# Rooms for every block of x, key and query weights on ScalarE's queue, chunks that end where blocks end

## The chip, the core and the metric

One core of a Trainium2 chip runs the kernel. The metric is device time of one execution in microseconds (us). The kernel before took 1500.04 us, the median of three runs (1497.89 to 1501.41).

TensorE (PE) does matmuls, VectorE (DVE) and GpSimd (POOL) elementwise work, ScalarE (ACT) copies, casts and activations; SyncE (SP) issues loads and stores, which 16 DMA engines carry out. Each engine works through its own list of instructions in order.

## The reference

Two layers over 1040 tokens (16 learned meta tokens, then 1024 of x) of width 1024; everything is float32.

```python
def hybrid_layer(h, ...):
    u = rms_norm(h, norm_g)
    proj = jnp.einsum('bld,dp->blp', u, w_in)          # 1024 x 4104
    dq, dk, dv, dz, fq, fk, fv, fz, f_logit = jnp.split(proj, split_points, axis=-1)
    # 4 differential heads: rope(q1), rope(q2), rope(k1), rope(k2), d = 64, v 128 wide
    #   p = softmax(q1 k1) - lam * softmax(q2 k2); o_a = rms_norm(p @ v_a) * (1 - lambda_init)
    # 8 forgetting heads, d = 64: softmax(q k / 8 + c_q - c_k) @ v, c = cumsum(log_sigmoid(f_logit + b))
    mixed = jnp.concatenate([o_a * jax.nn.silu(dz), o_b * jax.nn.silu(fz)], axis=-1)
    return h + jnp.einsum('bld,dm->blm', mixed, w_out)

out = rms_norm(h, final_g)[:, 16:]
```

## The kernel before, in words

**Precision.** A float32 product is made of three fast ones: each operand is split into a high part (a cast to fp32r) and the low rest. So a projection of one column block of 128 takes 24 matmuls per chunk of tokens: for each of the 8 slices of the width `XTh*whi`, `XTh*wlo` and `XTl*whi`. POOL splits weights (L314 high, L317 low, for quarters of 256 rows); ACT and DVE split x.

**The head of layer 0.** x is loaded in 8 blocks of 128 tokens (`hb`), block 0 being the 16 meta tokens. They are normed in three groups (`GRPS`: blocks 0 to 2, 3 to 5, 6 to 8): ACT squares each with a running sum (L256), DVE makes the factors of a group in a chain of small steps (L257, L231 to L244) and norms each block with the gain `gb` into `u` (L267). PE transposes `u` in halves (L282), ACT casts each half into `XTh` (L292), DVE subtracts the rest into `XTl` (L293).

**Unit 0.** Eight units (four differential heads, four pairs of forgetting heads) follow each other; unit 0's key, query and value projections (L341, L406) stand before its attention, and the next unit's projections are woven between its attention's steps by the scheduler. A projected key or query takes rope: ACT casts the chunk into `raw` (L491), SP copies its halves crosswise into `sw` (four copies, once for the first two chunks and once for the third), DVE multiplies by the cosine (L500), POOL `sw` by the sine (L501), DVE adds (L502), ACT and DVE split (L515, L508), and for the query SP copies the high part to the other half of the partitions (`qa`). The first matmul of an attention is L799 (meta tokens).

**Order and rooms.** Nobody writes the order: the framework's scheduler runs the program in a model of time and lists each engine's instructions by it. A tile names a tag with a number of rooms; where the rooms lie, and which earlier tile's place a new one takes, is decided in the same run, and the instruction that fills a tile then waits for the last readers of what lay there. `e` has 4 rooms and five blocks of x ask for one, so block 5 takes the room of block 1. Every load signals one of eight semaphores (DMAHW0 to 7), given in turn in that order, and waits until the load that had it before has landed.

SP's list begins with seven blocks of x, meta and gb, then `wf` (weights of the forget gates, 32 bytes a row), `gsc` (a small table), the key weights of unit 0 (L302, four quarters), its query weights (four), the rope tables, and block 5.

Of the kernel before, what the change touches and what calls it, by code (L numbers as in the profile page):

```python
# [12 lines left out]
F32 = mybir.dt.float32  # L13
# [6 lines left out]
P = 128  # L20
NM = 16
SEQ = 1024
L = NM + SEQ
D = 1024
KT = D // P
# [7 lines left out]
ST = 3  # L33
NE = 4
# [1 line left out]
MW = 584  # L36
AHEAD = 3
XORD = (1, 0, 2, 3, 4, 5, 6, 7, 8)
W0 = 8
ON_POOL = ()  # L40
SPL_POOL = ()
GRPS = ((0, 1, 2), (3, 4, 5), (6, 7, 8))
# [7 lines left out]
WLB = 6  # L50
VPB = 0
STB = 3
NQZ = 3
PMB = 4
OTB = 2
# [15 lines left out]
SH = 0  # L71
PP = ()
WARM = 20
CKB = False
KR = True
PG = ()
AQ = True
AV = True
WQ0 = False
WQ1 = False  # L80
CORD = (1, 0, 2, 3)
PSB = (0, 0, 0, 0)
Z_AT = {0: [0], 1: [1], 2: [2], 4: [3], 7: [4, 5, 6, 7]}
# [30 lines left out]
def hybrid_kernel(ctx: ExitStack, tc: tile.TileContext, x, meta, norm_g, w_in, b_forget,  # L114
                  lam_q1, lam_k1, lam_q2, lam_k2, subln_g, w_out, final_g, cos_t, sin_t, out):
    nc = tc.nc
# [5 lines left out]
    wp = Sized(ctx.enter_context(tc.tile_pool(name="wp", bufs=3)))  # L122
# [48 lines left out]
    def slot(nm):  # L171
        r = rings[nm]
        c = r[0] + r[3] % r[1] * r[2]
        r[3] += 1
        return cst[:, c:c + r[2]]
# [117 lines left out]
                nc.vector.tensor_tensor(out=lv, in0=psv, in1=hv.bitcast(F32), op=ALU.subtract)  # L293


    def load_w(l, col, q=None, room=None, rawroom=None):

        his, los = [], []
        raws = []
        for qt in range(4 if rawroom else 0):  # L300
            raws.append(rawroom(qt))
            (q or nc.sync).dma_start(out=raws[-1], in_=w_in[l, 256 * qt:256 * qt + 256, col:col + P].rearrange("(k p) c -> p k c", p=P))  # L302
        for qt in range(4):
          if rawroom:
            raw = raws[qt]
          else:
            raw = wp.tile([P, 2, P], F32, name="wraw", tag="wlo", bufs=WLB or None)
            (q or nc.sync).dma_start(out=raw, in_=w_in[l, 256 * qt:256 * qt + 256, col:col + P].rearrange("(k p) c -> p k c", p=P))
          if room is not None:
            hi, lo = room[:, qt], room[:, 4 + qt]  # L310
          else:
            hi = wp.tile([P, 2, P], F32R, name="whi", tag="whi", bufs=WHB or None)
            lo = None
          nc.gpsimd.tensor_scalar(out=hi, in0=raw, scalar1=1.0, scalar2=1.0, op0=ALU.mult, op1=ALU.mult)  # L314
          if lo is None:
            lo = wp.tile([P, 2, P], F32R, name="wlo", tag="wlo", bufs=WLB or None)
          nc.gpsimd.tensor_tensor(out=lo, in0=raw, in1=hi.bitcast(F32), op=ALU.subtract)  # L317
          his.append(hi)
          los.append(lo)
        return his, los  # L320
# [6 lines left out]
    ahead = {}  # L327
# [3 lines left out]
            late.pop(0)()  # L331

    def proj(l, col, chunks, evac):
        his, los = ahead.pop((l, col), None) or load_w(l, col, nc.scalar if (WQ1 and l == 0 and col % 512 == 0 and col < 2048) else None)
        for t0, n in chunks:
            ps = pj(f"pj_{l}_{col}")
            cnt = 0
            for k in range(KT):
                hi, lo = his[k // 2][:, k % 2, :], los[k // 2][:, k % 2, :]
                for w, xx in ((hi, XTh), (lo, XTh), (hi, XTl)):  # L340
                    nc.tensor.matmul(ps[:, :n], lhsT=w, rhs=xx[:, k, t0:t0 + n],  # L341
                                     start=(cnt == 0), stop=(cnt == 23))
                    cnt += 1
            run_late()
            evac(ps, t0, n)
            yield 24 * n / 2370.0
# [124 lines left out]
    def unit_proj(l, j, U, tabs):  # L471
        diff = j < 4
        cq, ck, cv, _ = unit_cols(j)
        tq = 0 if l == 0 else NM
        ch_q = CH_ALL if l == 0 else CH_REAL
        U.diff, U.j, U.l, U.tq = diff, j, l, tq
        lowhalf, tophalf = slice(0, 64), slice(64, 128)
        halves = (lowhalf, tophalf)
# [43 lines left out]
        def split_k(src, c0, scale, t0, n):  # L522
            for m in range(2):
# [1 line left out]
                hi = U.K1[m][halves[m], t0:t0 + n]  # L525
                hi_part(hi, x, scale)
                sub(U.K1[m][halves[1 - m], t0:t0 + n], x, scale, hi, f'k{m}')
        yield from project(ck, CH_BLK if CKB and l == 0 and j == 0 else CH_ALL, 0, 1.0, split_k)
        if not diff and KE:
            U.Kb = []  # L530
            for m in range(2):
# [409 lines left out]
    dma(bfb, bcast_rows(b_forget, P))  # L941
    hbs = {}
    gb = None
    htags = [("st", ST)] + [("e", NE)] * 5 + [("st", ST)] * 2 + [("ot", OTB)]
    for i, b in enumerate(XORD):
        t0, n = blk(b)
        tg, nb = htags[b]
        hb = big.tile([P, L], F32, name="hb", tag=tg, bufs=nb or None)[:, :D]
        dma(hb[:n], meta if b == 0 else x2[P * (b - 1):P * b])
        hbs[b] = (hb, n)  # L950
        if i == 0:
            gb = big.tile([P, L], F32, name="gb", tag="ot", bufs=OTB or None)[:, :D]
            dma(gb, bcast_rows(norm_g[0], P))
        if i == W0:
            ck0 = unit_cols(0)[1]
            ahead[0, ck0] = load_w(0, ck0, nc.scalar if WQ0 else None, None, (lambda qt: wp.tile([P, 2, P], F32, name="wraw", tag="wlo", bufs=WLB or None)) if KR else None)
    utags = ("k0", "k1", "qa0", "qa1") * 2 + ("ql",)
    for grp in GRPS:
        us = [stk.tile([P, L], F32, name="u", tag=utags[b])[:, :D] for b in grp]
# [9 lines left out]
    def prefetch(l, todo):  # L969

        for w in todo:
            col = unit_cols(0)["qkv".index(w)]
            if w == "k":
                ahead[l, col] = load_w(l, col)
            if w == "q":
                room = vp.tile([P, NB, 2, P], F32R, name="wroom", tag="V")
                ahead[l, col] = load_w(l, col, None, room,
                                       lambda qt: slot("es")[:, :256].rearrange("p (k c) -> p k c", k=2))
            if w == "v":
                ahead[l, "v"] = load_v01(l)  # L980

# [190 lines left out]
```

## Time and profile before

| | |
|---|---|
| median of three runs | 1500.04 us |
| the profiled execution | 1498.74 us |
| its span | 1497.1 us |
| PE busy | 1419.0 us, 95% |
| DVE, ACT, POOL busy | 955.3, 699.9, 627.8 us |
| L341 matmuls (projections) | 3 x 1392, about 452 us each third |
| chain that ended last | PE 75%, DVE 8%, DMA 5%, SP's queue 4% |

The span is cut into 40 slices of 37 us; the page's row of PE reads 28899..., so only the first slice shows PE mostly idle. A busy share over all 1497 us says nothing about that slice; it is read from its own rows below.

### The profile page before, as it was taken

How to read it: one execution, taken by the hardware profiler on the slowest of the kernel's cores; microseconds unless marked ns; L12 is line 12 of the kernel's file. 1: busy time of each engine (PE TensorE's matmuls, PEld its weight loads, DVE VectorE, ACT ScalarE, POOL GpSimd, SP SyncE). 2: the span in 40 equal slices, each digit the busy share in tenths (PEclk: the TensorE clock that was granted, in tenths of full speed). 3: DMA queues.
4: the chain of work that ended last, by engine and by line, in shares of the span. 5: the costliest groups of instructions: out<-in, count | busy, mean ns of one | idle time of the engine just before them, and what ended most of it. 6: DMA issues, size and time to landing. Idle time of an engine off the chain costs nothing.

```text
span 1497.1 us, 26781 instructions
## 1 busy us (share of the span) xinstructions
PE 1419.0 (95%) x9262; PEld 1348.8 (90%) x9262; DVE 955.3 (64%) x2721; ACT 699.9 (47%) x1729; POOL 627.8 (42%) x1118
## 2 busy tenths in 40 slices
PE   2889989899999999999999899899999999999997
PEld 2888989899999999997789899899999999999886
DVE  3548695957665656566564498867757555755653
ACT  3335554445454555456222365545445555654521
POOL 3525553633344444565106255435334454445500
PEclk7899999999999999999999999999999999999999
DMA  8314331332234224346434044224242323243632
GB/s 192 56 40 63 50 73 32 82 30 55 59 86 76 52 52 75 73 154 183 103 128 94 20 63 68 47 51 75 34 79 63 79 45 78 61 108 88 220 120 91
DMA packets 112280, 119.63 MB, mean 80 GB/s; under 512 B 15441, under 2 KB 92881, under 8 KB 112145
## 3 DMA queue, kind: packets, MB, share of 16 engines
q1 hardware_dynamic: 112144, 117.93, 36.2%
q8 instruction: 73, 1.20, 0.3%
q14 instruction: 63, 0.51, 0.1%
HBM read 70.92 MB, written 21.54 MB: 62 GB/s over the span
## 4 chain that ended last, share of the span: by engine, by line
PE 75%; DVE 8%; DMA 5%; SPq 4%; ACT 3%; issue 2%; POOL 2%; DVEq 0%; POOLq 0%; ACTq 0%
PE pj L341 36%; PE pss L1059 5%; PE pj L1059 5%; PE pss L679 4%; PE pt L854 4%; PE pss L681 4%; SPq L137 3%; PE pj L406 2%; PE po L788 2%; PE po L789 2%; DMA sw<-raw 2%; DMA wraw<-in_w_in_dram 2%; DVE E L685 2%; PE pt L1059 1%; POOL sw L501 1%
## 5 line engine op out<-in xcount | busy, mean ns | idle before, releaser
L341 PE MATMUL pj<-XTh,whi 128*128 128x346 f32 (+5 forms) x1392 | 454.7, 328 | 7.6 <-POOL whi L314 3.9
L341 PE MATMUL pj<-XTh,wlo 128*128 128x346 f32 (+5 forms) x1392 | 451.2, 325 | 3.6 <-POOL wlo L317 3.5
L341 PE MATMUL pj<-XTl,whi 128*128 128x346 f32 (+5 forms) x1392 | 450.4, 324 | 0.0
L341 PEld LDWEIGHTS pj<-XTh,whi 128*128 128x128 f32 x1392 | 263.0, 189 | 12.2 <-POOL whi L314 5.9
L341 PEld LDWEIGHTS pj<-XTh,wlo 128*128 128x128 f32 x1392 | 263.6, 189 | 6.2 <-POOL wlo L317 5.7
L341 PEld LDWEIGHTS pj<-XTl,whi 128*128 128x128 f32 x1392 | 263.3, 189 | 0.7 <-DVE XTl L293 0.3
L685 DVE CUSTOM_DVE_ANT_0 E<-pss,cst 128x456 f32<-128x456 f32 (+6 forms) x384 | 210.2, 557 | 68.6 <-PE pss L681 42.1
L692 ACT ACTIVATE E<-E,cst 128x400 f32<-128x400 f32 (+2 forms) x192 | 172.4, 898 | 137.2 <-DVE cst L685 130.5
L317 POOL TENSOR_TENSOR wlo<-wraw,whi 128x256 fp32r<-128x256 f32 x232 | 183.3, 790 | 65.7 <-PE pj L341 50.9
L763 DVE TENSOR_TENSOR ptl<-pt,pth 128x512 fp32r<-128x512 f32 (+1 forms) x240 | 150.2, 634 | 54.9 <-ACT pth L762 51.1
L314 POOL TENSOR_SCALAR whi<-wraw 128x256 fp32r<-128x256 f32 x232 | 106.7, 460 | 186.7 <-DMA wraw<-in_w_in_dram 156.6
L762 ACT CAST pth<-pt 128x512 fp32r<-128x512 f32 (+1 forms) x240 | 126.9, 543 | 92.9 <-PE pt L854 34.5
L679 PE MATMUL pss<-k,qa 128*128 128x400 f32 (+7 forms) x448 | 152.4, 345 | 10.0 <-DMA qa<-qa 5.0
L709 POOL TENSOR_SCALAR E<-E,cst 128x400 f32<-128x400 f32 (+2 forms) x96 | 83.8, 874 | 132.3 <-DVE cst L708 102.3
L662 POOL TENSOR_SCALAR XTl<-ql 64x128 fp32r<-64x128 f32 x136 | 50.8, 379 | 120.4 <-PE pss L681 95.6
L679 PEld LDWEIGHTS pss<-k,qa 128*128 128x128 f32 x448 | 85.0, 190 | 15.7 <-DVE cst L685 9.3
L854 PE MATMUL pt<-cst,E 128*128 128x128 f32 x576 | 88.0, 275 | 0.2
L788 PE MATMUL po<-pth,V 128*128 128x256 f32 x320 | 85.0, 286 | 0.0
L789 PE MATMUL po<-ptl,V 128*128 128x256 f32 x320 | 82.8, 287 | 0.0
L501 POOL TENSOR_TENSOR sw<-sw,sin 128x694 f32<-128x694 f32 (+3 forms) x32 | 51.0, 1595 | 57.2 <-DMA sw<-raw 51.4
L681 PE MATMUL pss<-k,XTl 128*128 128x400 f32 (+6 forms) x224 | 72.0, 327 | 0.0
L681 PE MATMUL pss<-k,q 68*128 68x400 f32 (+6 forms) x224 | 71.9, 325 | 0.0
(300 smaller groups left out, 2948.7 us busy)
## 6 DMA issues: line engine op xcount, KB each, us to landing
wraw<-in_w_in_dram SPq DMA_DIRECT2D x248, 128.0 KB
hb<-in_x_dram SPq DMA_DIRECT2D x16, 512.0 KB
wor<-in_w_out_dram SPq DMA_DIRECT2D x64, 128.0 KB
sw<-raw SPq DMA_DIRECT2D x48, 86.8 KB
ms<-OT SPq DMA_DIRECT2D x8, 520.0 KB
k<-k SPq DMA_DIRECT2D x16, 260.0 KB
h<-hb SPq DMA_DIRECT2D x8, 512.0 KB
ms<-OT SPq DMA_DIRECT2D x8, 512.0 KB
```

The lines of the kernel that those rows point to most:

```text
L317: nc.gpsimd.tensor_tensor(out=lo, in0=raw, in1=hi.bitcast(F32), op=ALU.subtract)
L341: nc.tensor.matmul(ps[:, :n], lhsT=w, rhs=xx[:, k, t0:t0 + n], start=(cnt == 0), stop=(cnt == 23))
L679: nc.tensor.matmul(ps[:, :nn], lhsT=U.Qa[m][:, t:t + P], rhs=U.K1[m][:, c0:c0 + nn], start=True, stop=False)
L681: nc.tensor.matmul(ps[:, :nn], lhsT=low[m], rhs=U.Kb[m][:, c0:c0 + nn], start=False, stop=True)
L685: nc.vector.tensor_tensor_reduce(out=E[:, c0:c0 + n], in0=ps[:, :n], in1=k, scale=-1.0, scalar=s[:, c - 1:c] if CHN and c else -NEG, op0=A ...
L692: nc.scalar.activation(E[:, :W], E[:, :W], AF.Exp, scale=-1.0, bias=lo, accum_out=s[:, 4:5])
L762: nc.scalar.copy(hi, ps)
L763: nc.vector.tensor_tensor(out=lo, in0=ps, in1=hi.bitcast(F32), op=ALU.subtract)
L788: nc.tensor.matmul(o[:, :256], lhsT=U.V[:, kb, hd, :], rhs=hi, start=False, stop=False)
L789: nc.tensor.matmul(o[:, :256], lhsT=U.V[:, kb, hd, :], rhs=lo, start=False, stop=last)
L854: nc.tensor.transpose(ps[:, (2 * a + b) * P:(2 * a + b + 1) * P], PP[:, k0:k0 + P], ident)
L1059: nc.tensor.matmul(ps, lhsT=xx[:, k, m0:m0 + P], rhs=wo[k][w][:, c], start=(k == 0 and i == 0), stop=(k == KT - 1 and i == 2))
```

## The change

Four settings and three pieces of code:

- `htags` gives block 5 a room of tag `k1` and block 8 one of tag `k0` (pool `stk`), so that no block of x takes another's place.
- `WQ0` and `W0`: the key weights of unit 0 are asked for right behind block 1 and issued by ACT, in two halves of 512 rows instead of four quarters, into one tile `wraw4` (tag `qa0`). `WQ1`: the query weights likewise (tag `qa1`), also by ACT.
- `CKB`: unit 0's key chunks end at block borders: 272, 384 and 384 columns (blocks 0 to 2, 3 to 5, 6 to 8) instead of 348, 346 and 346; its query chunks too in layer 0.

```diff
-W0 = 8
+W0 = 0
-CKB = False
+CKB = (0,)
-WQ0 = False
-WQ1 = False
+WQ0 = True
+WQ1 = True
...
-    def load_w(l, col, q=None, room=None, rawroom=None):
+    def load_w(l, col, q=None, room=None, rawroom=None, rawtag=None):
...
-        for qt in range(4 if rawroom else 0):
-            raws.append(rawroom(qt))
-            (q or nc.sync).dma_start(out=raws[-1], in_=w_in[l, 256 * qt:256 * qt + 256, col:col + P].rearrange("(k p) c -> p k c", p=P))
+        if rawroom == "half":
+
+            whole = stk.tile([P, L], F32, name="wraw4", tag=rawtag, bufs=STB or None)[:, :D].rearrange("p (k c) -> p k c", k=KT)
+            for a in (0, 4):
+                (q or nc.sync).dma_start(out=whole[:, a:a + 4], in_=w_in[l, P * a:P * a + 4 * P, col:col + P].rearrange("(k p) c -> p k c", p=P))
+            raws = [whole[:, 2 * qt:2 * qt + 2] for qt in range(4)]
+        elif rawroom:
+            for qt in range(4):
+                raws.append(rawroom(qt))
+                (q or nc.sync).dma_start(out=raws[-1], in_=w_in[l, 256 * qt:256 * qt + 256, col:col + P].rearrange("(k p) c -> p k c", p=P))
...
-        his, los = ahead.pop((l, col), None) or load_w(l, col, nc.scalar if (WQ1 and l == 0 and col % 512 == 0 and col < 2048) else None)
+        his, los = ahead.pop((l, col), None) or load_w(l, col)
...
-        ch_q = CH_ALL if l == 0 else CH_REAL
+        ch_q = (CH_BLK if j in CKB else CH_ALL) if l == 0 else CH_REAL
...
-        yield from project(ck, CH_BLK if CKB and l == 0 and j == 0 else CH_ALL, 0, 1.0, split_k)
+        yield from project(ck, CH_BLK if j in CKB else CH_ALL, 0, 1.0, split_k)
...
-    htags = [("st", ST)] + [("e", NE)] * 5 + [("st", ST)] * 2 + [("ot", OTB)]
+    htags = [("st", ST)] + [("e", NE)] * 4 + [("k1", STB)] + [("st", ST)] * 2 + [("k0", STB)]
...
-        hb = big.tile([P, L], F32, name="hb", tag=tg, bufs=nb or None)[:, :D]
+        hb = (stk if tg[0] == "k" else big).tile([P, L], F32, name="hb", tag=tg, bufs=nb or None)[:, :D]
...
-            ahead[0, ck0] = load_w(0, ck0, nc.scalar if WQ0 else None, None, (lambda qt: wp.tile([P, 2, P], F32, name="wraw", tag="wlo", bufs=WLB or None)) if KR else None)
+            ahead[0, ck0] = load_w(0, ck0, nc.scalar if WQ0 else None, None, "half", "qa0")
...
-                ahead[l, col] = load_w(l, col, None, room,
-                                       lambda qt: slot("es")[:, :256].rearrange("p (k c) -> p k c", k=2))
+                if l == 0:
+                    ahead[l, col] = load_w(l, col, nc.scalar if WQ1 else None, room, "half", "qa1")
+                else:
+                    ahead[l, col] = load_w(l, col, None, room,
+                                           lambda qt: slot("es")[:, :256].rearrange("p (k c) -> p k c", k=2))
```

What the scheduler makes of it, on two engines at the start of the program. SP's list before: `hb_158` is block 8, `hb_152` block 5, `cst_87 128x8x8` is wf, `wraw` and `cst_87 128x2x128` are quarters of the key and the query weights.

```order
L137 DMA hb_158<-in_x_dram 128x1024 [waits DMAHW0_49]
L137 DMA cst_87<-in_w_in_dram 128x8x8 [waits DMAHW1_49]
L137 DMA gsc_113<-in_subln_g_dram 128x8x1 [waits DMAHW2_49]
L302 DMA wraw_160<-in_w_in_dram 128x2x128 [waits DMAHW3_49]
...
L302 DMA cst_87<-in_w_in_dram 128x2x128 [waits DMAHW2_49]
L137 DMA cos_425<-in_rope_cos_dram 128x1040 [waits DMAHW3_49]
L137 DMA sin_426<-in_rope_sin_dram 128x1040 [waits DMAHW4_49]
L137 DMA bfb_114<-in_b_forget_dram 128x16 [waits DMAHW5_49]
L137 DMA hb_152<-in_x_dram 128x1024 [waits DMAHW6_49,DVE_49,Activation_49]
```

SP's list now: `hb_171` is block 5, `hb_173`, `hb_175` and `hb_177` are blocks 6 to 8, `wraw_387` the first quarter of value weights.

```order
L137 DMA hb_169<-in_x_dram 128x1024
L137 DMA hb_171<-in_x_dram 128x1024 [waits DMAHW0_49]
L137 DMA hb_173<-in_x_dram 128x1024 [waits DMAHW1_49]
L137 DMA hb_175<-in_x_dram 128x1024 [waits DMAHW2_49]
L137 DMA hb_177<-in_x_dram 128x1024 [waits DMAHW3_49]
L137 DMA cst_87<-in_w_in_dram 128x8x8 [waits DMAHW4_49]
L137 DMA gsc_113<-in_subln_g_dram 128x8x1 [waits DMAHW5_49]
L137 DMA wraw_387<-in_w_in_dram 128x2x128 [waits DMAHW6_49]
```

All blocks of x moved ahead of wf, gsc and the weights, and block 5 waits for DMAHW0 in place of DVE and ACT. DMAHW0 and DMAHW3 are signalled first by the two halves of the key weights on ACT's list, DMAHW1 and 2 by blocks 1 and 2.

ACT's list before, its squares of blocks 1, 2, 0, 3, 4, 6 (`hb_140` is block 1):

```order
L256 ACTIVATE u_185,cst_87<-hb_140 128x1024 [waits DMAHW0_49,DVE_49]
L256 ACTIVATE u_186,cst_87<-hb_146 128x1024 [waits DMAHW1_49]
L256 ACTIVATE u_184,cst_87<-hb_144 16x1024 [waits DMAHW2_49]
L256 ACTIVATE u_247,cst_87<-hb_148 128x1024 [waits DMAHW3_49]
L256 ACTIVATE u_248,cst_87<-hb_150 128x1024 [waits DMAHW5_49]
L256 ACTIVATE u_309,cst_87<-hb_154 128x1024 [waits DMAHW6_49]
```

ACT's list now, with the loads of the key weights ahead of it and the squares of blocks 1, 0, 3, 2, 4, 5:

```order
L304 DMA wraw4_144<-in_w_in_dram 128x4x128 x2
L943 ACT_TABLE_LOAD
L943 ACTIVATE cst_87<-cst_87 128x1 [waits DVE_49]
L256 ACTIVATE u_180,cst_87<-hb_140 128x1024 [waits DMAHW1_49,DVE_49]
L256 ACTIVATE u_179,cst_87<-hb_163 16x1024 [waits DMAHW4_49]
L256 ACTIVATE u_242,cst_87<-hb_167 128x1024 [waits DMAHW5_49]
L256 ACTIVATE u_181,cst_87<-hb_165 128x1024 [waits DMAHW2_49,DMAHW3_49,DMAHW0_49,Pool_49]
L256 ACTIVATE u_243,cst_87<-hb_169 128x1024 [waits DMAHW7_49]
L256 ACTIVATE u_244,cst_87<-hb_171 128x1024 [waits DMAHW0_49]
```

The square of block 2 moved behind that of block 3, and `u_181` lies where `wraw4_144` lies: it waits for both halves and for POOL, whose last split of the key weights reads them.

## Rows read from the trace of the kernel before

**Rows 1.** Busy us per engine and stretch; then granted clock, DMA share, GB/s.

```profile
0.00:42.45 42.45, 10.81 (x65) 10.19 (x65) 17.28 (x53) 14.04 (x28) 14.39 (x32) 0.70 0.79 170
42.45:81.12 38.67, 38.67 (x256) 37.89 (x256) 19.34 (x27) 12.59 (x25) 22.09 (x27) 0.94 0.35 64
81.12:87.03 5.91, 0.00 (x2) 0.03 (x1) 4.95 (x9) 2.63 (x7) 3.44 (x4) 0.82 0.52 145
87.03:125.00 37.97, 37.53 (x261) 37.20 (x262) 17.55 (x71) 12.30 (x44) 8.78 (x19) 0.94 0.10 23
```

**Rows 2.** Waits of PE, 0 to 130 us: total, times, longest.

```profile
PE pt L282 <- DVE u L267: 29.0, 3, 25.6
PE pss L799 <- DMA qa<-qa: 5.9, 1, 5.9
```

**Rows 3.** Timeline of SP's queue, 0 to 60 us: start, duration, load.

```profile
3.12 2.19 SPq L137 DMA_DIRECT2D hb<-in_x_dram  x4
...
11.74 4.72 SPq L302 DMA_DIRECT2D wraw<-in_w_in_dram  x4
...
30.97 0.61 SPq L137 DMA_DIRECT2D hb<-in_x_dram  x1
```

**Rows 4.** DMA: rates in 40 slices, 0:6 and 6:12; packets, 18:21 and 25:28.

```profile
GB/s 1 0 0 0 0 0 0 0 0 0 0 0 246 218 27 55 328 382 273 328 191 246 437 410 410 355 437 437 410 437 382 410 355 328 328 301 219 109 273 191
...
GB/s 191 273 382 410 410 410 437 410 328 355 273 300 273 273 355 300 218 382 355 410 437 410 410 437 437 410 437 410 382 410 410 437 382 382 410 437 437 437 410 382
...
DMA packets 275, 0.13 MB, mean 44 GB/s; under 512 B 17, under 2 KB 275, under 8 KB 275
...
DMA packets 755, 0.36 MB, mean 121 GB/s; under 512 B 44, under 2 KB 755, under 8 KB 755
```

**Rows 5.** Timeline of POOL, the last two splits of key weights.

```profile
28.20 0.41 POOL L314 TENSOR_SCALAR whi<-wraw 128x256 fp32r<-128x256 f32 x1 [1.83 <-DMA wraw<-in_w_in_dram]
...
30.39 0.72 POOL L317 TENSOR_TENSOR wlo<-wraw,whi 128x256 fp32r<-128x256 f32 x1
```

**Rows 6.** Timeline of ACT, squares of blocks 1 and 5.

```profile
4.57 1.06 ACT L256 ACTIVATE u<-hb 128x1024 f32<-128x1024 f32 x1 [2.27 <-DMA hb<-in_x_dram]
5.53 0.19 ACT L256 ACTIVATION_READ_ACCUMULATOR u<-hb 128x1 f32 x1
...
37.75 1.06 ACT L256 ACTIVATE u<-hb 128x1024 f32<-128x1024 f32 x1 [19.19 <-DMA hb<-in_x_dram]
```

**Rows 7.** Timeline of DVE: first small step, norms by group, last split.

```profile
8.52 0.17 DVE L257 TENSOR_SCALAR cst<-cst 128x3 f32<-128x3 f32 x1 [7.34 <-ACT u L256]
...
10.69 3.67 DVE L267 SCALAR_TENSOR_TENSOR u<-hb,cst,gb 16x1024 f32<-16x1024 f32 x3
...
20.82 3.81 DVE L267 SCALAR_TENSOR_TENSOR u<-hb,cst,gb 128x1024 f32<-128x1024 f32 x3
...
41.11 4.15 DVE L267 SCALAR_TENSOR_TENSOR u<-hb,cst,gb 128x1024 f32<-128x1024 f32 x3
...
58.53 0.69 DVE L293 TENSOR_TENSOR XTl<-pt,XTh 128x512 fp32r<-128x512 f32 x1 [1.17 <-ACT XTh L292]
```

**Rows 8.** Timeline of all engines: rope of unit 0, first attention matmul.

```profile
58.39 0.47 ACT L491 ACTIVATE raw<-pj 128x346 f32<-128x346 f32 x1
...
61.94 2.51 SPq L137 DMA_DIRECT2D sw<-raw  x4
...
67.45 2.04 POOL L501 TENSOR_TENSOR sw<-sw,sin 128x694 f32<-128x694 f32 x1 [1.63 <-DMA sw<-raw]
...
69.53 1.07 DVE L502 TENSOR_TENSOR raw<-raw,sw 128x694 f32<-128x694 f32 x1 [1.58 <-POOL sw L501]
...
70.68 1.57 ACT L515 CAST k<-raw 64x694 fp32r<-64x694 f32 x2 [6.08 <-DVE raw L502]
...
75.50 2.41 SPq L137 DMA_DIRECT2D sw<-raw  x4
...
87.03 0.35 PE L799 MATMUL pss<-k,qa 128*128 128x16 f32 x1 [5.91 <-DMA qa<-qa]
```

## The prediction

> **What bounds the kernel now.** I read first the table of busy time by stretch, then who waited for whom on TensorE (PE), then the queues that fed the waits. From 87 us on PE is busy all but 0.4 of 38 us, and it stays the engine with the least idle time to the end; in the first 42.45 us it has only 10.8 us of work, then it runs without a gap to 81.1 us, and then it stands for 5.9 us [rows 1]. PE waited for two things there: 29.0 us for normed blocks of x (25.6 us of it in one piece, up to 42.45), and 5.9 us for the copy of the first query (qa) [rows 2]. Instruction order behind the first attention is the same in both programs but for a handful of swaps, so the change is worth what it moves the start of that attention, L799 at 87.03 us [rows 8].
>
> Why the 25.6 us: block 5 of x shares its room with block 1. SP holds its load until the room is free and until all weight loads that stand before it in the queue have been issued; it goes out at 30.97 us [rows 3] and its square runs at 37.75 us [rows 6]. ScalarE (ACT) and VectorE (DVE) had everything else by 25 us. From 41.11 us the last three blocks are normed and transposed; the last split into XT ends at 59.2 us [rows 7]. From there a chain of rope steps leads to L799, 27.8 us later [rows 8].
>
> **What the change does to that wait.** Every block now has a room, so SP issues x in one go, and block 5's wait for block 1 is gone. But the rows of the new program show two new waits, and they, not the rooms, set the end. First, each load takes one of eight completion semaphores in turn and waits for the load that had it before. The two halves of the key weights, now on ACT's queue, took numbers 0 and 3: on SP block 5 waits until the first half has landed, block 8 until the second has, and behind them wait wf, gsc and the value weights. Second, the square of block 2 (u_181) waits for POOL: its output lies where the raw key weights lie. So ACT's squares of blocks 4 to 8 and the whole first group (its statistics on DVE, its three norms, all transposes) wait until POOL has split the second half of the key weights. The stage begins when these have landed; call that K.
>
> *K.* First packets move at about 2.2 us (slices of 0.15 us, steady from the 14th to 16th) [rows 4]. Each of the 16 DMA engines then has 64 packets of key weights (512 B) on ACT's queue, and on SP's 41 packets of x, meta and gb (4 KB), plus 24 more when the first half has landed. A 4 KB packet costs 160 ns (16 x 4096 B at 410 GB/s) [rows 4]. The trace never has two queues at once, so I bound. The same key weights took 16 x 3 us / 275 = 175 ns a packet when nothing else moved; the query weights behind them 16 x 3 / 755 = 64 ns [rows 4]. If the packets alternate and cost their sum, a pair is 335 or 224 ns. From the last packet to the reader it takes 1.1 us (block 1: 2.2 + 8 x 0.16 = 3.5 us, its square starts at 4.57 [rows 6]). So K = 2.2 + 64 pairs + 1.1: 24.7 us at 335 ns, 17.6 at 224, about 1 us less there since x pauses once. Under the lower bound lies the case that x hides behind the weights' waiting or waits for them: 64 x 0.175 + 3.3 = 14.5 us. I take 250 ns a pair, K = 19.3. It is nearer to the 64 ns row because the 175 ns row is a stretch with the engines busy but only 44 GB/s moving, which looks like a limit on scattered reads common to all engines, and such a limit is slack while x has every second turn.
>
> The Trainium skill ("DMA: Bandwidth & Descriptors", "Issuing engines are not separate DMA queues") says that loads issued by different engines run on the same 16 DMA engines and interleave, which saves only issue time. By that rule the weights gain nothing from their own queue and x pays for them in full: the first rival below. The same page ("Specifications") has 27 GiB/s per engine and line rate from 512 B on, so 18 ns for a packet; the trace has 64 to 175 ns, and the measurement decides.
>
> *From K to the first attention.* POOL splits the second half: two at 0.41 and two at 0.72 us [rows 5], 2.3 us. Block 2's square and its sum cost 1.06 + 0.19 [rows 6]; 0.3 us for the hops. So the first group is released at S = K + 3.85. DVE then has nearly all of its work of the stage before it: three chains of small steps of 2.17 us (8.52 to 10.69), norms of 3.67 + 2 x 3.81, sixteen splits of 0.69 and two small ones (11.3), and 1.1 us of small steps for wf and gsc, 30.2 us in all [rows 7]; I add 2.1 us of gaps, mostly for the first 24 projection matmuls, which stand on PE ahead of block 3's transposes. The last split ends at S + 32.3. ACT (nine squares, sixteen casts of about 0.55) and PE (transposes and two chunks of the key) lie beside it. Blocks 6 to 8, wf and gsc are needed by S + 8 and land by K + 6: hidden.
>
> The chunk sizes help at the end. Chunk 2 of the key needs blocks 0 to 5 only and is cast at S + 29.8, 2.5 us before the last split; in the trace it was done at 58.86, 0.4 us before it. There SP was held by the next unit's weights until 61.94 [rows 8]; now all eight value weights have rooms of their own and that wait is gone. Then with the trace's durations [rows 8]: four copies out and landed 5.5, POOL 2.0, DVE 1.1, two casts 1.6, chunk 3's cast 0.5 behind them: S + 40.5. Its own copies about 4.7 and POOL and DVE about 1.0 and 0.6, for 384 columns in place of 656: S + 46.8, when the query's copies may start; from there 75.50 to 87.03 = 11.5 us. L799 starts at S + 58.2. PE has its projections and the first 64 value matmuls done at about S + 53.3, so it still waits some 5 us; V does not set the start.
>
> *The sum.* L799 at K + 3.85 + 58.2 against 87.03: the gain is 25.0 - K. With K = 19.3 it is 5.7 us. Every pair costs the same columns as before (272 + 384 + 384 = 348 + 346 + 346), also in layer 1, where CKB holds too; its last rope chunk grows by 38 columns, a tenth of a 1 us step, taken as nothing. Rooms later in the kernel move with the new allocation; with the order kept I put that at 0, within 1.5 us either way. The profiled execution took 1498.74 us, 1.6 over its span and 1.3 under the median of 1500.04; from the median I get 1494.3 us.
>
> **Rivals.** (1) *The queues only take turns, and the weights stay slow*: a pair at 335 ns, K = 24.7, gain 0.3, 1499.7 us. For it: 175 ns was measured on these very bytes, and the rule above. Against: the query's loads had the same shape and took a third. (2) *The weights come early*: K of 14 to 17, gain 8 to 11, about 1490.5 us. For it: SP's gate on block 5 leaves x short of packets, in the weights' favour. Against: the 175 ns. (3) *Slower*: the weights make x's packets slower too, so that a pair costs over 0.38 us and K passes 28; then block 2's square holds ACT, DVE and PE past the time at which block 5 held them. At 0.42 us a pair, K = 30.2 and the time is 1505.2; it decides from K = 28. Against: a pair would have to cost more than both its parts at their dearest. (4) The rooms do nothing: excluded by the order, where no load of x waits for a square any more.
>
> **How the numbers follow.** Forecast, K of 17 to 22: 0.42. Weights early: 0.24. Slow weights, K of 22 to 28: 0.26. Slower: 0.08. About 0.2% (3 us) can be told from no change, which is K = 22 on one side and K = 28 on the other: faster 0.65 (the first two, less a little for the later rooms), same 0.27, slower 0.08. The range goes from K = 13 (1488) to K = 25.5 with a us of layout (1501.5).
>
> **What would show it.** The POOL row of the fourth split of whi gives K: 17 to 22 us. Block 2's square starts 2.3 us after, as the fourth square, with POOL or a weight load as its releaser. PE's long wait for u ends near 27 to 30 us instead of 42.45; the last split near 55, L799 near 81, still behind a wait for qa of some 5 us. The step from K to L799 is wrong if L799 - K is not 60 to 64 us. The prediction is wrong if K lies outside 14 to 25, if wf or gsc hold DVE, or if a gain at L799 is not found again in the span.

## The result, and the profile after

The changed kernel took 1491.26 us, the median of five runs (1486.17 to 1493.52), against 1501.31 us (1497.89 to 1503.97) of five runs of the kernel before: ratio 0.9932 [0.991, 0.9954], faster by 6.9 to 13.5 us. The forecast was 1494.3, range 1488.0 to 1501.5, with 0.65 on faster. The two profiled executions took 1498.74 and 1493.05 us, their spans are 1497.1 and 1491.3. The first attention starts at 81.42 us instead of 87.03, 5.6 earlier, and what follows lasts 1409.9 us instead of 1410.1: in the traced pair the whole gain lies in the head of the program.

Busy time by stretch, up to the first transposes, from there to the end of PE's wait for `raw` (the copied chunk of a projected key), and from there to the first attention (columns as in [rows 1]; the last three are granted clock, DMA share and GB/s):

```profile
0.00:25.23 25.23, 7.20 (x41) 7.01 (x41) 3.41 (x16) 8.85 (x15) 7.61 (x22) 0.79 0.94 204
25.23:49.51 24.28, 16.21 (x94) 14.58 (x94) 19.66 (x48) 9.10 (x22) 12.05 (x18) 0.78 0.70 125
49.51:81.42 31.91, 30.22 (x186) 29.66 (x187) 15.20 (x21) 11.26 (x23) 19.77 (x23) 0.91 0.31 69
```

PE is mostly idle in the first stretch as before (7.2 us of work), but that ends 17 us sooner than the 42.45 us of [rows 1]. In exchange PE is only two thirds busy in the second stretch, where before, from 42.45 us on, it ran without a gap. Its waits in the first 130 us, which answer to [rows 2]:

```profile
PE pt L282 <- DVE u L267: 15.6, 2, 15.4
PE pt L282 <- ACT raw L498: 5.1, 1, 5.1
PE pss L806 <- DMA qa<-qa: 1.5, 1, 1.5
```

The 25.6 us for block 5 are gone. 15.4 us for the first norms have come, and 5.1 us for ACT's copy of a projected chunk, which the forecast did not have. SP's queue, for [rows 3] (start, duration, load):

```profile
0.81 0.87 SPq L137 DMA_DIRECT2D hb<-in_x_dram  x2
1.72 0.43 SPq L137 DMA_DIRECT2D hb<-in_meta_tokens_dram  x1
2.19 3.92 SPq L137 DMA_DIRECT2D hb<-in_x_dram  x1
...
8.02 10.49 SPq L137 DMA_DIRECT2D hb<-in_x_dram  x5
```

The second and the fifth of the last five, blocks 5 and 8, one by one:

```profile
10.66 2.98 SPq L137 DMA_DIRECT2D hb<-in_x_dram  x1
...
18.19 0.33 SPq L137 DMA_DIRECT2D hb<-in_x_dram  x1
```

No load of x stands behind weights in SP's list any more, yet the last five leave between 8.0 and 18.5 us. Blocks 5 and 8 leave just as the two halves of the key weights land (POOL begins to split them at 10.72 and 18.25 us), by the semaphores that the prediction names; block 8 waited about 2 us for that. The rest is slow issue: blocks 4 and 5 took SP 2.50 and 2.98 us. And what had been issued did not move. The DMA engines by queue, for [rows 4]: q1 carries SP's loads, q10 ACT's, that is the key weights. The stretches 4 to 6, 6 to 8 and 10 to 12 us (packets, MB, share of 16 engines):

```profile
q10 hardware_dynamic: 134, 0.07, 99.0%
q1 hardware_dynamic: 6, 0.02, 2.0%
...
q10 hardware_dynamic: 137, 0.07, 101.7%
...
q10 hardware_dynamic: 167, 0.08, 54.1%
q1 hardware_dynamic: 101, 0.36, 51.3%
```

Where the first half of the key weights moves, x stands still: 134 packets of 512 B in 2 us over 16 engines are about 237 ns each, beside six packets of x. Block 2 and meta had been issued by 2.2 us. From 9 us on the two share the engines, until the second half holds them again at 12 us. What this does to ACT, DVE and POOL up to the first norm, for [rows 5 to 7] (timelines):

```profile
18.25 0.78 POOL L321 TENSOR_SCALAR whi<-wraw 128x256 fp32r<-128x256 f32 x2 [5.38 <-DMA wraw<-in_w_in_dram]
...
18.99 1.41 POOL L324 TENSOR_TENSOR wlo<-wraw,whi 128x256 fp32r<-128x256 f32 x2
...
17.53 1.05 ACT L256 ACTIVATE u<-hb 16x1024 f32<-16x1024 f32 x1 [11.03 <-DMA hb<-in_meta_tokens_dram]
...
19.51 1.06 ACT L256 ACTIVATE u<-hb 128x1024 f32<-128x1024 f32 x1 [0.83 <-DMA hb<-in_x_dram]
...
20.57 1.04 ACT L256 ACTIVATE u<-hb 128x1024 f32<-128x1024 f32 x1
...
21.73 0.17 DVE L257 TENSOR_SCALAR cst<-cst 128x3 f32<-128x3 f32 x1 [20.54 <-ACT u L256]
```

The second half of the key weights is there at 18.25 us (K of the prediction). Meta, issued at 1.72 us, is squared at 17.53, block 3 at 19.51; block 2 is the square at 20.57. POOL's last split had ended at 20.40, and ACT went from block 3's square to block 2's without idle time, so both bounds came due together. From there to the first attention, for [rows 7, 8]:

```profile
42.08 1.83 POOL L321 TENSOR_SCALAR wroom<-wraw 128x256 fp32r<-128x256 f32 x2 [3.67 <-DMA wraw<-in_w_in_dram]
...
47.63 1.40 POOL L377 TENSOR_TENSOR vwl<-wraw,vwh 128x256 fp32r<-128x256 f32 x2
...
49.06 0.40 ACT L498 ACTIVATE raw<-pj 128x272 f32<-128x272 f32 x1 [8.96 <-POOL vwl L377]
...
53.86 0.49 ACT L498 ACTIVATE raw<-pj 128x384 f32<-128x384 f32 x1 [2.61 <-PE pj L348]
...
56.19 1.29 DVE L293 TENSOR_TENSOR XTl<-pt,XTh 128x512 fp32r<-128x512 f32 x2 [0.16 <-ACT XTh L292]
...
81.42 0.25 PE L806 MATMUL pss<-k,qa 128*128 128x16 f32 x1 [1.53 <-DMA qa<-qa]
```

ACT stood 8.96 us before the copy of the first key chunk, until POOL had split value weights; `raw` now lies where two raw quarters of these lie, and POOL stood behind the query weights, which came at 42.08 us.

### The profile page after: what moved, and what is told of

Read it like the earlier page. It is cut to its first block, busy times and chain, and to the rows that moved or that the text cites. A ratio compares the mean times of both kernels' runs of the same rounds, so it can differ in the third digit from the quotient of the medians.

```text
span 1491.3 us, 26753 instructions
## 1 busy us (share of the span) xinstructions
PE 1424.5 (96%) x9262; PEld 1353.5 (91%) x9262; DVE 955.4 (64%) x2721; ACT 699.3 (47%) x1729; POOL 630.7 (42%) x1118
## 4 chain that ended last, share of the span: by engine, by line
PE 74%; DVE 9%; DMA 7%; issue 3%; ACT 3%; POOL 2%; SPq 1%; DVEq 0%; POOLq 0%; ACTq 0%
PE pj L348 35%; PE pss L1069 5%; PE pj L1069 5%; PE pss L686 4%; PE pt L861 4%; PE pss L688 3%; DMA wraw<-in_w_in_dram 3%; PE pj L413 2%; PE po L795 2%; PE po L796 2%; DVE E L692 2%; PE pt L1069 1%; SPq L137 1%; DMA sw<-raw 1%; DMA hb<-in_x_dram 1%
## 5 line engine op out<-in xcount | busy, mean ns | idle before, releaser
L508 POOL TENSOR_TENSOR sw<-sw,sin 128x694 f32<-128x694 f32 (+5 forms) x32 | 52.6, 1643 | 68.8 <-DMA sw<-raw 65.8
```

## The experiments

All times are medians in us. Each ratio is against runs of the kernel before that were taken with them; their medians lay between 1499.41 and 1501.58 us, so rows are compared by their ratios. "Start" is the first attention in the profile, "rest" what follows it in the span.

| run | median | ratio, 95% | start | rest |
|---|---|---|---|---|
| before | 1501.31 | | 87.03 | 1410.1 |
| after | 1491.26 | 0.9932 [0.991, 0.9954] | 81.42 | 1409.9 |
| e1 rooms alone | 1486.83 | 0.9917 [0.9904, 0.9929] | 74.4 | 1410.5 |
| e2 without the rooms | 1497.81 | 0.9994 [0.9984, 1.0003] | 86.97 | 1412.2 |
| e3 old chunks | 1496.48 | 0.9985 [0.9976, 0.9995] | 84.32 | 1408.6 |
| e4 key weights elsewhere | 1489.83 | 0.9938 [0.9926, 0.995] | 79.69 | 1405.5 |
| e5 rooms and chunks | 1485.07 | 0.9892 [0.9872, 0.9911] | 74.0 | 1411.7 |
| e6 key weights on SP | 1488.66 | 0.9919 [0.9901, 0.9937] | 80.22 | 1410.5 |
| e7 key and query weights in quarters | 1489.2 | 0.993 [0.9913, 0.9947] | 79.62 | 1406.8 |
| e8 query weights late | 1491.24 | 0.9937 [0.9924, 0.995] | 78.09 | 1411.6 |
| e9 e5, query weights late | 1484.56 | 0.9898 [0.9882, 0.9914] | 71.89 | 1408.8 |
| e10 e9, wf first | 1486.62 | 0.9907 [0.9894, 0.992] | 75.94 | 1409.0 |
| e11 e9, wf by ACT | 1488.11 | 0.991 [0.9892, 0.9927] | 75.51 | 1412.1 |
| e12 e10, gsc first too | 1486.09 | 0.9911 [0.9895, 0.9926] | 74.49 | 1411.5 |

The rest varies from 1405.5 to 1412.2 us with no order that follows the edits, so a start tells the time to about 3 us, and smaller differences are read from the traces alone.

**e1, the rooms alone** (in the kernel before):

```
-    htags = [("st", ST)] + [("e", NE)] * 5 + [("st", ST)] * 2 + [("ot", OTB)]
+    htags = [("st", ST)] + [("e", NE)] * 4 + [("k1", STB)] + [("st", ST)] * 2 + [("k0", STB)]
...
-        hb = big.tile([P, L], F32, name="hb", tag=tg, bufs=nb or None)[:, :D]
+        hb = (stk if tg[0] == "k" else big).tile([P, L], F32, name="hb", tag=tg, bufs=nb or None)[:, :D]
```

> The kernel before with one part of the change: rooms of their own for blocks 5 and 8. Key and query weights stay on SP's queue, now behind all of x; chunks stay 348, 346, 346. Theory A (the start of the first attention is set by when the squares and norms of x can run; the queue of the weights matters only through that): x goes out in one piece and lands by about 14 us, the first group is released at about 8.5 us as before, DVE needs 30.2 us plus gaps, so the last split of XT ends at 41 to 47 us (57.5 in the changed kernel, 59.2 before); the key weights land at about 22 to 24 us, so PE starts its projections there, has some 46 us of work from then on, and the first attention starts at 75 to 80 us: 6 to 12 us earlier than before, a time of 1488 to 1494 us, at least as good as the whole change. Rival B (the gain comes from the early start of the weights in ACT's queue): without it rooms alone give at most 1 to 2 us, the first attention at 85 to 87 us, the time 1496 to 1501 us.

The start came at 74.4 us, 7.0 before the changed kernel's, and the time at 1486.83. PE's first attention matmul, SP's queue (start, duration, load), then DVE's last split:

```profile
74.37 0.25 PE L799 MATMUL pss<-k,qa 128*128 128x16 f32 x1 [2.27 <-DMA qa<-qa]
```

```profile
3.12 3.06 SPq L137 DMA_DIRECT2D hb<-in_x_dram  x5
6.22 5.67 SPq L302 DMA_DIRECT2D wraw<-in_w_in_dram  x4
```

```profile
49.54 0.69 DVE L293 TENSOR_TENSOR XTl<-pt,XTh 128x512 fp32r<-128x512 f32 x1 [1.16 <-ACT XTh L292]
```

Five loads of x leave in 3.1 us here, in 10.5 in the changed kernel. Theory B falls, at the start and in time. A's windows were missed too: the last split ended at 50.2 us, 3 later than its latest, while start and time came a little earlier than its earliest. At the start one part of the change is worth more than the whole; in time the two intervals (0.9904 to 0.9929 and 0.991 to 0.9954) overlap.

**e2, the changed kernel without the rooms** (its `htags` line as before).

> The changed kernel with one part undone: blocks 5 and 8 ask for their rooms as before, so block 5's load stands behind the rope tables again and waits for a norm. Theory A: that load goes out at 28 to 31 us, its square runs at 34 to 38 us, the second group's norms and transposes with blocks 3 to 5 come last, PE waits in one piece of 5 us or more for a normed block, and the first attention starts 3 to 7 us later than in the changed kernel (81.4 us): 1494 to 1498 us. Rival B: rooms are not what pays; the first attention within 1 us of 81.4, the time within 1 us of the changed kernel's.

Block 5's load left at 28.96 us (SP's queue), its square came at 42.30 (ACT's timeline), later than the 37.75 of [rows 6]:

```profile
28.96 1.97 SPq L137 DMA_DIRECT2D hb<-in_x_dram  x1
```

```profile
42.30 1.06 ACT L256 ACTIVATE u<-hb 128x1024 f32<-128x1024 f32 x1 [11.52 <-DMA hb<-in_x_dram]
```

The start is 86.97 us, as before the change, and the ratio's interval holds 1: the weights' queue and the chunks together bring nothing that can be told without the rooms.

**e3, the old chunks** (`CKB = ()` for `(0,)`).

> The changed kernel with one part undone: unit 0's key and query chunks are 348, 346 and 346 again. Theory A, by the forecast's sum: the second key chunk then waits for blocks of the third group (2.5 us later) and the last copies and steps of rope cover 346 columns in place of 384; in the changed kernel's trace PE waits only 1.5 us for the query there, so the first attention starts 0 to 3 us later, time 0 to 3 us more. Rival C (the borders are what pays): 4 us or more is lost, the first attention at 85 us or later.

The start moved 2.9 us, as A said and near the 2.5 of the prediction, and did not reach C's 85. The time does not agree: from 0.9932 to 0.9985 are 8 us, where A allowed 3 and C asked for 4 or more. The traced execution, at 1494.6 us, was among the fastest of the twelve, so what the chunks are worth in time stays open between 3 and 8 us.

**e4, the raw key weights away from block 2's square** (`"half", "ql"` for `"half", "qa0"`).

> The changed kernel with the raw key weights in another room (tag ql in place of qa0), so that the square of block 2 no longer waits for POOL's split of them; the last block's square waits for POOL instead, which has long been done. Theory A with the split of the key weights as the limit: the first group is released when its last block has landed. In the changed kernel the meta block landed at 17.5 us and block 3 at 19.5 us, behind the key weights of the other queue, so the group starts at 18 to 20.5 us in place of 21.7; PE gets its first transposes 1 to 3.5 us earlier. At the first attention at most 1 us of it is left, because the copy of the first key chunk out of PSUM still waits for POOL, which waits for the query weights (42.1 us): time within 1 us of the changed kernel. Rival (the wait of block 2's square sets everything behind it): the first attention moves by the same 2 to 3.5 us, 1488 to 1490 us.

PE's first transposes, DVE's first small step of the group, then ACT's square of meta:

```profile
24.29 1.03 PE L282 MATMUL pt<-cst,u 16*128 16x16 f32 x8 [14.12 <-DVE u L267]
...
19.94 0.53 DVE L257 TENSOR_SCALAR cst<-cst 128x3 f32<-128x3 f32 x1 [18.76 <-ACT u L256]
```

```profile
18.76 1.05 ACT L256 ACTIVATE u<-hb 16x1024 f32<-16x1024 f32 x1 [4.36 <-DMA hb<-in_meta_tokens_dram]
```

The group began at 19.94 us in place of 21.73, as A said, but the transposes came only 0.9 us earlier and the start 1.7, outside both theories' windows; the ratio is the changed kernel's within its interval. Taking the wait for POOL away uncovers the load of meta, which was as late.

**e5, rooms and chunks, weights left on SP's queue** (e1 with `CKB = True` and `CH_BLK` for layer 0's first query).

> The kernel before with two of the three parts: the rooms for blocks 5 and 8, and unit 0's key and query chunks of layer 0 ending at block borders. What is left out against the changed kernel is ScalarE's queue: key and query weights come in quarters on SP behind all of x. Rooms alone put the first attention at 74.4 us and the time at 1486.8 us; the old chunks in the changed kernel cost 2.9 us at the first attention. Theory A2 (formed after the first four runs: rooms and borders pay, the weights' own queue costs, since x is starved while they move): first attention at 70 to 75 us, time 1482 to 1488 us, so 3 to 9 us under the changed kernel's 1491.3. Rival B2 (the queue pays once the chunks end at block borders, so the three belong together): not better than the changed kernel, 1490 us or more, the first attention at 80 us or later.

Start 74.0, time 1485.07: as A2 said. Against e1 the chunks bring 0.4 us at the start, where they brought 2.9 in the changed kernel (e3). The weights also stay in quarters and in their old rooms here, and the key's new chunks hold for layer 0 alone, so the 7.4 us to the changed kernel are those of the own queue with all that came with it, the weights' earlier place among the loads first of all (e6).

**e6, the key weights back on SP at their new place** (`WQ0 = False`).

> The changed kernel with one part undone: the key weights' two halves are issued by SP, behind the meta block and behind block 4, in place of ScalarE; the query weights stay on ScalarE's queue. Block 2's square waits for no weights, block 6's does. Theory A2: blocks 0 to 2 land by 6 to 8 us and the first group is released at 8 to 9 us in place of 21.7; the key weights land at 17 to 21 us, about as in the changed kernel, the copy of the first key chunk still waits for POOL behind the late query weights (42 us in the changed kernel), so the first attention starts at 74 to 79 us in place of 81.4: 1484 to 1489 us. Rival B2: the second half of the key weights lands at 25 us or later without a queue of its own and PE has nothing to project until then, so the first attention is at 81 us or later and the time 1491 us or more.

PE's first attention matmul, a wait of DVE and one of ACT (total, times, longest), and the one queue that moves from 6 to 8 us:

```profile
80.22 0.25 PE L806 MATMUL pss<-k,qa 128*128 128x16 f32 x1 [1.30 <-DMA qa<-qa]
...
DVE u L267 <- DMA gb<-in_norm_g_dram: 5.2, 1, 5.2
...
ACT raw L498 <- POOL vwl L377: 13.1, 1, 13.1
...
q1 hardware_dynamic: 149, 0.08, 103.9%
```

The time lies in A2's window and the start (80.22) 1.2 us behind it, 0.8 short of B2's. The first group's squares came early, but gb stood behind the first half of the weights, and ACT's wait for `raw` grew to 13.1 us. Weights between the blocks of x starve x in one queue as in two: with their place kept, the own queue is worth nothing at the start (81.42 against 80.22).

**e7, the key and the query weights in four loads of 256 rows**, still by ACT:

```
-            for a in (0, 4):
-                (q or nc.sync).dma_start(out=whole[:, a:a + 4], in_=w_in[l, P * a:P * a + 4 * P, col:col + P].rearrange("(k p) c -> p k c", p=P))
+            for a in (0, 2, 4, 6):
+                (q or nc.sync).dma_start(out=whole[:, a:a + 2], in_=w_in[l, P * a:P * a + 2 * P, col:col + P].rearrange("(k p) c -> p k c", p=P))
```

> The changed kernel with the key and query weights of unit 0 asked for in four loads of 256 rows each in place of two of 512, still by ScalarE; the scheduler then lets block 6's square wait for POOL, not block 2's. In the changed kernel block 2 of x moved only when the second half of the key weights began (9 to 12 us) and the meta block only when that was done (17.5 us). Theory A3 (the two queues take turns by whole loads: one load of x passes with each load of weights): block 2 lands by 7 to 9 us, the meta block by 9 to 12 us and block 3 by 13 to 16 us, the key weights still at 16 to 19 us; the first group is released at 10 to 13 us, and the first attention starts at 75 to 80 us. Rival A4 (packets of the weights go ahead of x for as long as there are any): block 2 and the meta block land at 16 us or later whatever the size of the loads, the first group is released at 18 us or later, and the first attention moves by less than 2 us. Rival A5 (packets alternate one by one): x lands in proportion from the start, block 3 by 8 us.

ACT's squares of blocks 2, meta and 3, DVE's first norms, then the queues from 6 to 8 us:

```profile
9.08 1.06 ACT L256 ACTIVATE u<-hb 128x1024 f32<-128x1024 f32 x1 [6.29 <-DMA hb<-in_x_dram]
...
11.96 1.05 ACT L256 ACTIVATE u<-hb 16x1024 f32<-16x1024 f32 x1 [0.69 <-DMA hb<-in_meta_tokens_dram]
...
16.22 1.06 ACT L256 ACTIVATE u<-hb 128x1024 f32<-128x1024 f32 x1 [3.10 <-DMA hb<-in_x_dram]
...
20.23 3.66 DVE L267 SCALAR_TENSOR_TENSOR u<-hb,cst,gb 16x1024 f32<-16x1024 f32 x3 [4.31 <-DMA gb<-in_norm_g_dram]
```

```profile
q1 hardware_dynamic: 118, 0.45, 60.2%
q10 hardware_dynamic: 100, 0.05, 42.9%
```

In the changed kernel q1 moved no packet in that stretch. With loads half as large x comes twice as often, in the three windows that A3 named or at their edge; by these rows A4 (16 us or later) and A5 (block 3 by 8 us) fall. The start gained 1.8 us only, which A4 allowed too, since DVE then waited for gb until 20.2 us; the ratio (0.993) did not move.

**e8, the query weights back behind the key** (`PF0 = "v"` for `"qv"`).

> The changed kernel with one setting more: the query weights of unit 0 are not fetched ahead (PF0 = "v"), so they are loaded by SP in four quarters behind the value weights, and POOL splits the value weights before them. It is aimed at the wait that the forecast did not have: in the changed kernel ACT's copy of the first key chunk out of PSUM waits 9.0 us (to 49.06) for POOL, whose split of the value weights stands behind the query weights that land at 42.1 us, and PE stands 5.1 us behind it. Theory A6 (that wait is worth its PE idle): the copy runs at 39 to 43 us, PE's 5.1 us go, the last split of XT ends at 51 to 54 us in place of 57.5, the query weights are split by 50 to 54 us, before PE asks for them, and the first attention starts at 76 to 79 us in place of 81.4: 1485.5 to 1489 us. Rival B6 (the wait hides nothing, since the end is set by the chain of rope copies or by the query weights, now later): the first attention within 1.5 us of 81.4 or later, 1490 us or more.

ACT's copy of the first key chunk:

```profile
41.82 0.40 ACT L498 ACTIVATE raw<-pj 128x272 f32<-128x272 f32 x1 [4.74 <-POOL vwl L377]
```

It stands 7.2 us earlier, the wait is 4.2 us shorter and the start 3.3 earlier, so the trace follows A6. The time did not: 1491.24 us, a ratio of 0.9937, lies outside A6's window and inside B6's. The rest is 1.7 us longer in this trace; whether the gain at the start reaches the time is not shown.

**e9, e5 and e8 together.**

> The kernel with rooms and block-sized chunks, all weights on SP (first attention 74.0 us, 1485.1 us), with the same setting: the query weights not ahead of the value weights but behind them. There DVE waited 5.7 us for wf, which stood in the queue behind and among the weights, ACT waited 8.8 us with the first key chunk for POOL, and PE 4.3 us for the copied query. Theory A6: wf comes right behind the key weights, so DVE's wait for it shrinks to 0 to 3 us, the copy of the first key chunk waits under 4 us, and the first attention starts at 69 to 73 us: 1480 to 1484.5 us, the best of all. Rival B6: the query's weights, now last in the queue, hold PE: PE waits 3 us or more for POOL's split of them and the first attention stays at 73.5 us or later, 1485 us or more.

PE's first attention matmul, and DVE's wait for wf (its tile is named `cst`):

```profile
71.89 0.25 PE L799 MATMUL pss<-k,qa 128*128 128x16 f32 x1 [1.01 <-DMA qa<-qa]
```

```profile
DVE vwh L360 <- DMA cst<-in_w_in_dram: 6.2, 1, 6.2
```

The earliest start and, with e5, the lowest time. The intervals of e1, e5 and e9 to e12 all overlap, so these can't be told apart by time; that of e9 (0.9882 to 0.9914) just overlaps the changed kernel's (0.991 to 0.9954). The time lies at the upper edge of what A6 gave, and the wait for wf did not shrink as expected: it was 5.7 us in e5.

**e10, wf ahead of the key weights; e11, wf first and by ACT; e12, wf and gsc ahead** (all from e9). The load of wf becomes a function of its own, `load_wf`, called where the key weights are asked for and ahead of them; e11 calls it with ACT's queue; e12 is e10 with gsc's load moved from the program's head to behind it:

```
+            wfs[0] = load_wf(0)
...
+            wfs[0] = load_wf(0, nc.scalar)
...
-        dma(gsc, subln_g.rearrange("l (h p) -> p l h", p=P))
+            dma(gsc, subln_g.rearrange("l (h p) -> p l h", p=P))
```

> The best kernel so far (rooms, block-sized chunks, all on SP, query weights late: first attention 71.9 us, 1484.6 us) with wf asked for ahead of the key weights on SP. DVE waited 6.2 us for wf there, behind it the norms of blocks 3 to 5; PE waited 5.8 us for POOL's splits. Theory A7 (DVE's queue is what holds the stage now): the wait for wf falls under 1 us, the key weights land 1.5 to 3.5 us later because wf's 1024 packets of 32 bytes go first, and the first attention starts at 69 to 71.5 us, 1480.5 to 1484 us. Rival B7 (the key weights hold PE, so what DVE gains PE loses): 71.5 us or later, 1484 us or more.

> The same kernel with wf asked for first of all by ScalarE, in a queue of its own, while x moves on SP's queue. It tries the sharing of the queues with another kind of load: 32-byte packets in place of 512-byte ones. Theory A3 (a turn is a whole load): block 1 moves with wf, then wf has to end before more of x than one load goes on, so blocks 2 and 0 land 1 to 3 us later than without it (squares at 6.3 and 7.3 us there), not more, since there is only one such load; x goes on alone after that. Then DVE's wait for wf is gone and the key weights come no later: first attention at 68 to 71.5 us, 1479.5 to 1484 us. Rival (packets of a second queue always go first and hold x for as long as it has any, with 1024 packets): the same 1 to 3 us; the two are not told apart by this run unless x moves during wf. Rival B7: first attention 71.5 us or later.

> The kernel with wf ahead of the key weights, and gsc, the other small load that DVE waited for (7.8 us in that run), right behind wf and ahead of the key weights too. Theory A8 (DVE, which runs its list in order, stands at whichever small load is late, with the norms of blocks 3 to 5 behind it): the wait for gsc falls under 2 us, PE's waits for normed blocks fall from 7.1 us to 2 to 4, and the first attention starts at 69 to 73 us in place of 75.9: 1480 to 1485 us. Rival B8 (the key weights, now behind two small loads, take the place of the wait): PE's waits for POOL's splits grow from 7.2 us to 9 or more and the first attention stays at 74 us or later, 1485 us or more.

In e10 DVE's wait only moved one load down its list, and PE waited 7.2 us for the key weights' splits:

```profile
DVE gsc L221 <- DMA gsc<-in_subln_g_dram: 7.8, 1, 7.8
...
PE pj L341 <- POOL wlo L317: 4.5, 3, 2.9
PE pj L341 <- POOL whi L314: 2.7, 2, 1.6
```

In e11 block 2's square slipped from 6.07 us (e9) to 8.23, and the queues shared the engines, here from 4 to 5 us, so that x moved beside wf and the rival by which a second queue always goes first fits badly:

```profile
q1 hardware_dynamic: 28, 0.10, 33.3%
q10 hardware_dynamic: 561, 0.02, 28.9%
```

In e12 DVE's waits for wf and gsc are gone, and PE's for the key weights' splits grew to 11.3 us:

```profile
PE pj L340 <- POOL whi L313: 6.8, 2, 5.3
PE pj L340 <- POOL wlo L316: 4.5, 4, 2.5
```

A7 falls and B7 holds; of A8 the waits came true and the start did not, and B8's numbers are met. Starts of 75.94, 75.51 and 74.49 us are all later than e9's 71.89: in each case what was moved back became the next wait.

## Why the prediction was right

*Block 5's wait goes, and another ends the idle time sooner.* Right in kind. PE's long wait ended at 25.23 us, 2 us before the forecast "near 27 to 30". It ended 3.5 us after S (below), so the forecast's own S gives 25.6.

*K.* Forecast 19.3, measured 18.25: (18.25 - 3.3) / 64 = 234 ns a pair, for 250. The size holds and the picture under it doesn't. I let packets alternate and gave x "every second turn", so that a packet of weights was cheap. The rows show turns by whole loads: 237 ns a packet of weights with x standing still, then x (e7). The sum came out by luck: a pair at 234 ns was the price of the weights alone. Two readings of [rows 4] were loose as well. The rate rises at the 17th slice, 2.4 us, and the 64 ns mix the end of the key weights with faster packets: from 26 us on 672 packets passed in 2 us, 48 ns each.

*S.* Forecast 22.1 by K + 3.85, measured 21.73. Block 2's square came 2.3 us behind K as the fourth, as foreseen, but the loads of meta and block 3 held ACT just as long (e4), a wait that the prediction did not have.

*The last split.* Forecast S + 32.3 = 54.0, measured 56.19 + 1.29 = 57.5. Here a step failed: "I add 2.1 us of gaps", together with "all eight value weights have rooms of their own and that wait is gone". SP's wait went, but `raw` had taken a place among these weights, and the wait came back on ACT: 8.96 us there, 5.1 on PE. The second chunk's cast, S + 29.8 = 51.5 by the forecast, came 2.3 us late, at 53.86. I had followed the rooms of what was loaded, not what else lay in them. e8 shows the size: with the query weights later, `raw` moved by 7.2 us and the start by 3.3.

*From the second chunk on.* Forecast 28.4 us from its cast to the first attention, measured 81.42 - 53.86 = 27.6. PE's last wait for qa was 1.5 us instead of "some 5", which fits the 5.1 us it had stood at `raw`; that the one replaced the other is argued, not shown.

*The sum.* With the measured K, 25.0 - K is 6.75; the start moved 5.6. From K to the first attention 63.2 us were measured for 62.05. So two errors of about a us cancel, the late `raw` against the early K, and the forecast 5.7 stands nearer to 5.6 than its steps deserve. The rest, 0 within 1.5, measured -0.2. The chunks' 2.5 us measured 2.9 at the start (e3), with the own queue; without it 0.4 (e5 against e1).

*The rivals.* K of 18.25 is the forecast's case. Neither slow weights (K from 22) nor early ones (up to 17) nor the slower case (from 28) came. Of the rule in the Trainium skill ("DMA: Bandwidth & Descriptors", "Issuing engines are not separate DMA queues") the runs here bear out that loads of both issuing engines draw on the same 16 DMA engines (shares of 54.1 and 51.3% from 10 to 12 us). That a second issuer saves no more than issue time fits e6, where the start is 80.22 us without it and 81.42 with it. "Interleave" must be read as by whole loads here (e7).

*Not seen beforehand.* The rooms alone give the earlier start, by 7.0 us. The prediction priced the own queue only by when its weights arrive; what weights ahead of x take from it was a term that it did not set against the kernel with rooms and the weights behind x.

*Open.* The medians differ by 10.0 us, the interval begins at 6.9, and the traced pair holds 5.7 us. Before's profiled execution lies 2.6 us under its median and after's 1.8 above, which makes up the difference; where those few us arise, no trace here shows.

## What to carry to other kernels

What the first stage reads should move first and alone: weights for a later stage, asked for among its loads, were paid for by the first stage, load by load, on a second queue as on the same one (e6). Smaller loads let x through sooner (e7), but the time did not move by it. When a tile gets a room of its own, follow what else now lies there, on every engine: the wait removed from SP came back on ACT. Moving one late small load ahead in an engine's in-order list hands the wait to the next one (e10, e12), so the whole list is counted before it is moved.

## What the runs showed of the hardware

A 512 B packet of key weights took 175 ns when nothing else moved [rows 4] and 237 ns with loads of x waiting in another queue, though x hardly moved in that time. That the second queue makes the difference is not shown: in e6, where one queue moved, the same halves took about 223 ns from 6 to 8 us (149 packets at 103.9%). Loads of x that had been issued by 2.2 us stood until a load of weights was through (9 us and 16 us), and with loads half as large they moved twice as often (e7). SP's issue stretched meanwhile: 2.50 and 2.98 us for blocks 4 and 5, against 3.06 for five loads (e1). A load of 32 B rows on the second queue (wf, e11) shared the engines with x at 28.9 and 33.3%, where the first half of the key weights left x 2.0%.
